# Dealing a routing stage's score products among other tiles, with a shorter per-layer gate, in a two-layer encoder kernel

## The chip, the cores and the metric

The kernel runs on one core of a Trainium2 chip. Its time is the device time of one execution in microseconds (us). The engines run side by side, each through its own queue in order: TensorE (PE, with its weight loads as PEld), VectorE (DVE), ScalarE (ACT), GpSimd (POOL) and SyncE (SP), which issues nearly all DMAs.

## What is computed

Two layers over 256 tokens of width 1024. Layer 0 mixes with a Mamba-2 block, layer 1 with retention; each is followed by a PEER expert FFN and a gated per-layer input. All matrices are float32. The FFN and the gate matter here:

```python
def peer_ffn(h, w_q, sub_keys, u, v):            # h: rms-normed
    q = (xt @ w_q).reshape(T, PEER_HEADS, 2, PEER_HALF)
    sc = jnp.einsum('thcd,hckd->thck', q, sub_keys)
    s1, i1 = lax.top_k(sc[:, :, 0], K)
    s2, i2 = lax.top_k(sc[:, :, 1], K)
    cand = (s1[..., :, None] + s2[..., None, :]).reshape(T, PEER_HEADS, K * K)
    ...
    gate = jax.nn.softmax(top_s, axis=-1)
    hid = jax.nn.gelu(jnp.einsum('tkd,td->tk', u[ib], xb), approximate=False)
    return jnp.einsum('tk,tkd->td', (gb * hid), v[ib])

h = h + peer_ffn(rms_norm(h, ffn_norm[i]), ...)
g = jax.nn.sigmoid(rms_norm(h, ple_norm[i]) @ ple_gate[i])
h = h + g * (p[i] @ ple_proj[i])
```

There are 16384 experts, 8 heads, 128 keys in each half and K = 16. The kernel doesn't gather experts: it multiplies all tokens with all of u, multiplies by a dense matrix of gates (zero where an expert isn't chosen), and multiplies with all of v.

## The kernel before

Every float32 product is made of three products in float32r: each operand is split into a high part (`wh`, `xh`: a cast on ScalarE) and the rest (`wl`, `xl`: a subtraction on VectorE or GpSimd). `get()` hands out the next split weight tile; it also starts the cast of the tile after that and the load of one further on. `wh` and `wl` have two buffers each, so a cast waits until TensorE is through with the tile two before.

The stages of a layer are the mixer, `peer` and `ple`. The program is written in the order in which each engine shall work; nothing reorders it.

`peer` runs these stages:

- Two q products of eight steps (`dense`), 1024 columns of q each. After a step `dense` calls a function with the step's number: in the second product `q_fill`, which issues a part of the selection (`pump`, 1550 ns of credit), moves x between partitions by DMA (steps 0 and 1) and splits x for the u tiles (steps 4 and 6). At the end four banks are evicted by VectorE (`q_evac`, L353).
- Scores: `score(tb, c4)` multiplies four of the 16 key halves for a block of 128 tokens into one PSUM tile (of two, `g`), and ScalarE copies it out (L995). Two of the eight calls stand between the two products, for q of the first product; six stand behind the second.
- The selection (`bg`, a list of pieces with costs): `sel_codes` takes the top 16 of two key halves on VectorE, for token block 0 and then block 1; sums, candidates, positions and gates follow, and at last `sel_tr`, which turns the gates on TensorE.
- u: 128 tiles. A tile's 128 rows are loaded, transposed by VectorE (L511), cast by ScalarE (L516), split by GpSimd (L519), and used in 24 products (L1237 to L1241) into a PSUM tile (of two, `m`). The loop issues selection pieces (`PUMP`) until the list is empty. From then on each tile also has a gate slot: `g_hot` (VectorE) and `g_lo` (ScalarE) make one-hot operands for four tokens, `g_mm` (L1183) multiplies them, `g_apply` (L1195, L1193) puts the gates of these tokens for all 128 tiles into `H`, and `gelu` (L1201, L1204, L1205) joins the activation to them. There are 64 such groups of four tokens.
- v: 128 steps (L1266). Four rows of `H` at once are split by `wsplit` into the operands for four steps.

`ple` forms p's projection (`pp`, scaled by 0.5), then the product with `ple_gate` (`dense` with `ends=2`: the last two steps run bank by bank, L213), with the norm's pieces issued from the table `FIRST_PLE` ("q", "Q", "t", "s": squares, sum, spread). The sigmoid is 0.5 + 0.5 tanh: `base` (L1335) adds `pp` to h on GpSimd during the product, `gated` (L1339) multiplies the tanh by `pp`, `added` (L1343) adds to h. Bank 0's `gated` and the first two `added` run on GpSimd, the others on VectorE.

Of the kernel before, what the change touches and what calls it, by code (L numbers as in the profile page):

```python
# [8 lines left out]
F32 = mybir.dt.float32  # L9
# [5 lines left out]
OP = mybir.AluOpType  # L15
# [3 lines left out]
P = 128  # L19
T = 256  # L20
# [4 lines left out]
GS = 4096.0  # L25
PUMP = 1700
UEND = 56
HPOOL = (0, 1)
GPOOL = (0,)

# [16 lines left out]
FIRST_SSD = ('aq', 't', 's', '', '0h', '1H', 'b', '')  # L49
FIRST_RET = ('', 'qQ', '', 'cbt', 'das0', '', 'h1', 'H')  # L50
FIRST_Q = ('q', 'Q', '', 't', 'sa', 'b', '', '')
FIRST_PLE = ('q', 'Q', '', 't', 'sa', 'bcd', '', '')
HEADS = 8
TOPK = 16

# [32 lines left out]
def trunk(ctx: ExitStack, tc: tile.TileContext, a, out, dbg=None, stop=None):  # L88
    nc = tc.nc
    pe, act, dve, pool, sp = nc.tensor, nc.scalar, nc.vector, nc.gpsimd, nc.sync  # L90
# [12 lines left out]
    hT = big.tile([P, KD, T], F32, name="hT")  # L103
# [17 lines left out]
    def place():  # L121
        v = X[:, xn[0] % 3]
        xn[0] += 1
        return v[:, 0], v[:, 1]
# [58 lines left out]
    def split_x(src, n=4):  # L183

        xh, xl = place()
        act.copy(xh[:, :n], src)  # L186
        dve.tensor_sub(xl[:, :n], src, xh[:, :n].bitcast(F32))
        return xh, xl
# [30 lines left out]
    def dense(xs, evac, pieces=lambda k: 0, m=2, ends=1):  # L219


        s = Acc()
        for k in range(KD - 2 if ends == 2 else KD):
            if xs is st0:
                xs.before(k)
            wh, wl = get()
            if isinstance(xs, Stream) and xs is not st0:
                xs.before(k)
            xh, xl = (xs.xs if isinstance(xs, Stream) else xs)[k]
            s.step(wh, wl, xh, xl, k == 0, m if k == KD - 1 else 0)  # L230
            if k < KD - 1:
                fill(pieces(k))
        if ends == 2:
            s.close([get(k < KD - 1) + xs.xs[k] for k in (KD - 2, KD - 1)])
        for b in range(4):
            evac(b, s.bank(b))
        fill(pieces(KD - 1))
# [143 lines left out]
    def first(st, xs, plan, *more):  # L381


        named = {"q": (st.squares, 0), "Q": (st.squares, 2), "t": (st.total,), "s": (st.spread,),
                 "0": (st.scaled, 0, xs), "h": (st.half, 0, xs), "1": (st.scaled, 1, xs), "H": (st.half, 1, xs)}
        for i, c in enumerate(more):
            named["abcdef"[i]] = c

        def f(k):
            todo[:0] = [named[c] for c in plan[k]]  # L390
            return len(plan[k])

        return f
# [552 lines left out]
    def peer(l, st):  # L946
        H = view(0, P, T)
# [41 lines left out]
        def score(tb, c4):  # L989
            ps = gps.tile([P, 512], F32, name="g")  # L990
            for j in range(4):
                c = 4 * c4 + j
                pe.matmul(ps[:, j * P:(j + 1) * P], qT[:, c, tb * P:(tb + 1) * P], kT[:, c], start=j == 0,
                          stop=True, skip_group_check=True)
            act.copy(sc[:, tb, 4 * c4:4 * c4 + 4], ps.rearrange("p (a b) -> p a b", a=4))  # L995
# [110 lines left out]
        def wait():  # L1106
            pass

        bg = [(3100, sel_codes, tb, c) for tb in range(2) for c in range(0, 16, 2)]
        for tb in range(2):  # L1110
            bg += [(1800, sel_sums, tb)]
            bg += [(2500, sel_cand, tb, h) for h in range(0, 8, 2)]
# [14 lines left out]
                fn(*x)  # L1127

        def q_fill(k):
            if bg[0][3] < 8:  # L1130
                pump(1550)
            if k < 2:
                q_move(2 * k)
                q_move(2 * k + 1)
            if k in (4, 6):
                xh, xl = split_x(xm[:, 2 * k - 8:2 * k - 4])
                xp.extend((xh[:, i], xl[:, i]) for i in range(4))
            return 0

        dense(st, q_evac(0), first(st, None, FIRST_Q, (normed, 0), (normed, 1)))  # L1140
        score(0, 0)
        score(0, 1)
        dense(st.xs, q_evac(8), q_fill)

        for c4 in (2, 3):
            score(0, c4)
        for c4 in range(4):
            score(1, c4)


        bank = [acc.tile([P, 512], F32, name="ps") for _ in range(4)]
# [35 lines left out]
        def g_apply(b, ps, i):  # L1187

            pv = ps.rearrange("p (t i) -> p i t", t=4)
            assert i >= UEND  # L1190
            hv = H[:, :, 4 * b:4 * b + 4]
            if i < P:
                act.activation(hv[:, i:], pv[:, i:], AF.Copy, scale=1.0 / GS)  # L1193
            if i:
                dve.scalar_tensor_tensor(hv[:, :i], pv[:, :i], 1.0 / GS, hv[:, :i], op0=OP.mult, op1=OP.mult)  # L1195
            stored[0] = 4 * b + 4

        def gelu(i, ps):
# [25 lines left out]
        for i in range(P):  # L1224
            wh, wl = get()
            if last is not None:
                g_slot(i, gelu(i - 1, last))
                if bg:
                    pump(PUMP)
                else:  # L1230
                    since += 1
                    if since % 8 == 0 and T // 4 - gst["next"] > P - 1 - i:
                        g_slot(i)
            last = mis.tile([P, 512], F32, name="m")[:, :T]
            for k, (xh, xl) in enumerate(xp):
                s = slice(k * P, (k + 1) * P)
                pe.matmul(last, wh[:, s], xh, start=k == 0, stop=False)  # L1237
                pe.matmul(last, wh[:, s], xl, start=False, stop=False)  # L1238
            for k, (xh, xl) in enumerate(xp):
                s = slice(k * P, (k + 1) * P)  # L1240
                pe.matmul(last, wl[:, s], xh, start=False, stop=k == KD - 1)  # L1241
        assert not bg

        def wsplit(j):
            return split_x(H[:, 4 * j:4 * j + 4])

        def open_():
            return gst["next"] < T // 4 or gst["lo"] or gst["mm"] or gst["ap"]
# [46 lines left out]
        pp = view(0, KD, T)  # L1295
# [28 lines left out]
    def ple(l, st, pp):  # L1324
        ga = view(2560, KD, T)
        st2 = Stream(COL["mix_norm"] + 8)
        if l:
            gfin, junk = view(16384, D), view(17408, T)
            fs = small.tile([P, 2, 4], F32, name="fs", bufs=1)
            sp.dma_start(gfin, a["final_norm"].partition_broadcast(P))  # L1330


        def base(b):
            hv = hT[:, 2 * b:2 * b + 2]
            pool.tensor_add(hv, hv, pp[:, 2 * b:2 * b + 2])  # L1335

        def gated(b):
            g = ga[:, 2 * b:2 * b + 2]
            (pool if b in GPOOL else dve).tensor_mul(g, g, pp[:, 2 * b:2 * b + 2])  # L1339

        def added(b):
            hv = hT[:, 2 * b:2 * b + 2]
            (pool if b in HPOOL else dve).tensor_add(hv, ga[:, 2 * b:2 * b + 2], hv)  # L1343
            if l == 0 and b < 3:
                st2.hi(2 * b)
                st2.hi(2 * b + 1)

        def turned_out(b):

            for tb in range(2):  # L1350
                o = ot[b // 2 * 2 + tb][:, b % 2 * T:b % 2 * T + T]
                for k in range(2):
                    pe.transpose(o[:, k * P:(k + 1) * P], hch[2 * b + k][:, tb * P:(tb + 1) * P], ident)
            for tb in range(2):
                o = ot[b // 2 * 2 + tb][:, b % 2 * T:b % 2 * T + T]
                act.activation(junk[:, :T], o, AF.Square, accum_out=fs[:, tb, b:b + 1])

        def g_evac(b, ps):
            g = ga[:, 2 * b:2 * b + 2]
            st.divide(g, ps)  # L1360
            if b == 3:
                prepare(True)
            act.activation(g, g, AF.Tanh, scale=0.5)
            if b == 1:
                gated(0)
            if b == 2:
                added(0)
                gated(1)
            if b == 3:
                added(1)  # L1370
                gated(2)

        if l == 0:
            keys = view(30464, 4, 512)
            for c4 in range(4):
                key_load(1, c4, keys[:, c4])
        dense(st, g_evac, first(st, None, FIRST_PLE, *((base, b) for b in range(4))), ends=2)
        if l == 0:
            tiles = [pool_.tile([P, 512], F32, name=n_) for pool_, n_ in ((gps, "g"), (gps, "g"), (mis, "m"), (mis, "m"))]
            for c4 in range(4):  # L1380
                key_turn(keys[:, c4], tiles[c4])
            st2.copies = [(key_copy, c4, tiles[c4]) for c4 in range(4)]
            st2.lo(0)
            st2.lo(1)
            ready.append(ready.pop()())
            prepare(True)
            added(2)
            gated(3)
            added(3)
            return st2  # L1390
        ot = [pool_.tile([P, 512], F32, name=n_) for pool_, n_ in ((gps, "g"), (gps, "g"), (mis, "m"), (mis, "m"))]
        added(2)
        turned_out(0)
        gated(3)
        added(3)
        for b in range(1, 4):
            turned_out(b)
        return ot, fs, gfin
# [26 lines left out]
    for j in range(2):  # L1425
        for tb in range(2):
            o = raws.tile([P, D], F32, name="raw")[:, :512]
            c = slice(512 * j, 512 * j + 512)
# [29 lines left out]
```

## Time and profile before

| | us |
|---|---|
| Runs shown | 2243.55, 2245.3, 2249.71 |
| Median | 2245.3 |
| Profiled execution | 2246.1 |
| Its span | 2244.2 |
| TensorE busy | 2165.3 (96%) |
| TensorE weight loads | 2006.2 (89%) |
| VectorE busy | 1563.2 (70%) |
| ScalarE busy | 1210.4 (54%) |
| GpSimd busy | 878.4 (39%) |

Durations in the rows come from the profiled execution. Its span runs from the first to the last instruction of the program, the 1.9 us around it belong to the execution. "Busy" is time in which an instruction of the engine ran; what an engine waited for is a view of its own. Layer 0's second q product begins at 299.18 us of the span, its u tiles at 332.69, v at 756.89; layer 1's u tiles begin at 1421.57, v at 1843.32.

### The profile page before, as it was taken

The numbers are of one execution on the slowest core, as the hardware profiler recorded it, in microseconds if no ns is written. First come the engines' busy times: TensorE is split into PE (matmuls) and PEld (weight loads), VectorE is DVE, ScalarE is ACT, GpSimd is POOL, SyncE is SP. The second block draws the span as 40 slices with busy tenths as digits, with TensorE's granted clock in tenths as the row PEclk, the third lists the DMA queues.
The fourth block names the chain that finished last, engine by engine and source line by source line (L and its number), as shares of the span: only waits on it lengthen the run. The fifth ranks groups of instructions, "written<-read, shape, count | busy, mean of one in ns | idle before, by whom it ended". The sixth has DMA issues, their size and how long they took to land. (4 is left out here: it accounts for less than half of the span.)

```text
span 2244.2 us, 39809 instructions
## 1 busy us (share of the span) xinstructions
PE 2165.3 (96%) x15013; PEld 2006.2 (89%) x15013; DVE 1563.2 (70%) x2625; ACT 1210.4 (54%) x2063; POOL 878.4 (39%) x408
## 2 busy tenths in 40 slices
PE   7899899999999999999989999999999999999997
PEld 7788899999999888888888999999999998888886
DVE  7478678887788655555587366889678875555556
ACT  4544444546888644444553444445588874444444
POOL 5743248886666200000044123788766640000002
PEclk9999999999999999999999999999999999999998
DMA  5432467756555555555645455776555545666653
GB/s 165 136 106 86 143 192 181 183 139 160 143 148 144 160 195 190 196 193 192 201 160 174 138 166 177 176 191 154 160 148 145 145 147 194 193 194 192 194 192 104
DMA packets 219577, 370.27 MB, mean 165 GB/s; under 512 B 24240, under 2 KB 163192, under 8 KB 219384
## 3 DMA queue, kind: packets, MB, share of 16 engines
q1 hardware_dynamic: 219064, 367.19, 55.0%
q8 instruction: 118, 1.93, 0.4%
q14 instruction: 75, 0.61, 0.1%
q10 hardware_dynamic: 320, 0.53, 0.1%
HBM read 364.48 MB, written 1.05 MB: 163 GB/s over the span
## 5 line engine op out<-in xcount | busy, mean ns | idle before, releaser
L135 ACT CAST wh<-raw 128x1024 fp32r<-128x1024 f32 x429 | 450.3, 1052 | 519.7 <-PE ps L1266 362.5
L138 DVE TENSOR_TENSOR wl<-raw,wh 128x1024 fp32r<-128x1024 f32 x365 | 453.6, 1246 | 393.9 <-ACT wh L135 393.9
L519 POOL TENSOR_TENSOR wl<-raw,wh 128x1024 fp32r<-128x1024 f32 x256 | 615.5, 2406 | 240.5 <-ACT wh L516 231.1
L1266 PE MATMUL ps<-wh,X 128*128 128x512 f32 x2048 | 509.2, 390 | 4.6 <-ACT X L186 4.6
L1237 PE MATMUL m<-X,wh 128*128 128x256 f32 x2048 | 512.9, 288 | 0.6 <-ACT arena L1201 0.6
L1238 PE MATMUL m<-X,wh 128*128 128x256 f32 x2048 | 501.8, 283 | 0.0
L1266 PEld LDWEIGHTS ps<-wh,X 128*128 128x128 f32 x2048 | 385.0, 188 | 85.3 <-ACT X L186 5.0
L516 ACT CAST wh<-raw 128x1024 fp32r<-128x1024 f32 x256 | 269.1, 1051 | 274.9 <-issue 157.1
L1237 PEld LDWEIGHTS m<-X,wh 128*128 128x128 f32 x2048 | 392.8, 192 | 1.2 <-ACT arena L1201 1.0
L1238 PEld LDWEIGHTS m<-X,wh 128*128 128x128 f32 x2048 | 391.2, 191 | 0.0
L198 PE MATMUL ps<-X,wh 128*128 128x256 f32 x2368 | 333.6, 291 | 14.7 <-ACT wh L135 8.4
L340 POOL TENSOR_TENSOR arena<-arena 128x512 f32<-128x512 f32 x15 | 22.5, 1502 | 825.2 <-ACT arena L338 824.8
L198 PEld LDWEIGHTS ps<-X,wh 128*128 128x128 f32 x2368 | 307.5, 197 | 20.7 <-ACT wh L135 10.4
L1241 PE MATMUL m<-X,wl 128*128 128x256 f32 x2048 | 287.4, 283 | 0.1
L1266 PE MATMUL ps<-wl,X 128*128 128x512 f32 x1024 | 274.7, 389 | 0.0
L1241 PEld LDWEIGHTS m<-X,wl 128*128 128x128 f32 x2048 | 264.1, 191 | 0.7 <-POOL wl L519 0.7
L1266 PEld LDWEIGHTS ps<-wl,X 128*128 128x128 f32 x1024 | 192.4, 188 | 40.1
L138 POOL TENSOR_TENSOR wl<-raw,wh 128x1024 fp32r<-128x1024 f32 x64 | 165.5, 2597 | 157.6 <-ACT wh L135 157.5
L511 DVE STREAM_TRANSPOSE raw<-raw 128x1024 f32<-128x1024 f32 x144 | 179.2, 1244 | 50.1 <-DMA raw<-in_peer_u 37.4
L198 PE MATMUL ps<-X,wl 128*128 128x256 f32 x1184 | 178.9, 289 | 15.6 <-POOL wl L138 8.0
L198 PEld LDWEIGHTS ps<-X,wl 128*128 128x128 f32 x1184 | 159.6, 196 | 18.0 <-DVE wl L138 9.0
L1177 ACT ACTIVATE ol<-oh,G 128x128 f16<-128x128 f16 x512 | 168.4, 401 | 1.5 <-PE g L1183 0.3
(263 smaller groups left out, 2158.9 us busy)
## 6 DMA issues: line engine op xcount, KB each, us to landing
raw<-in_peer_v SPq DMA_DIRECT2D x256, 512.0 KB, 4.3
raw<-in_peer_u SPq DMA_DIRECT2D x576, 128.0 KB, 3.0
arena<-in_peer_u SPq DMA_DIRECT2D x448, 128.0 KB, 3.3
raw<-in_ret_w_in SPq DMA_DIRECT2D x48, 512.0 KB, 4.1
raw<-in_ssd_w_in SPq DMA_DIRECT2D x41, 512.0 KB, 3.7
raw<-in_peer_w_q SPq DMA_DIRECT2D x32, 512.0 KB, 4.8
raw<-in_ssd_w_out SPq DMA_DIRECT2D x16, 512.0 KB, 3.6
raw<-in_ple_gate SPq DMA_DIRECT2D x16, 512.0 KB, 4.5
```

What stands on the lines that cost most here:

```text
L135: act.copy(wh[:, :n], r[:, :n])
L138: (eng or dve).tensor_sub(wl[:, :n], r[:, :n], wh[:, :n].bitcast(F32))
L198: pe.matmul(self.t[n // 2][:, n % 2], w[:, n * P:(n + 1) * P], x, start=st, stop=sp_, skip_group_check=True)
L340: pool.tensor_add(self.sq[:, 0], self.sq[:, 0], self.sq[:, b])
L511: dve.transpose(t.rearrange("p (k b i) -> p b k i", k=8, b=4), r.rearrange("p (b k i) -> p b k i", k=8, b=4))
L516: act.copy(wh, t)
L519: pool.tensor_sub(wl, t, wh.bitcast(F32))
L1177: act.activation(ol[:, j], oh[:, 0, :, j], AF.Copy, scale=G1[:, t:t + 1])
L1237: pe.matmul(last, wh[:, s], xh, start=k == 0, stop=False)
L1238: pe.matmul(last, wh[:, s], xl, start=False, stop=False)
L1241: pe.matmul(last, wl[:, s], xh, start=False, stop=k == KD - 1)
L1266: pe.matmul(sums[b], h[:, tb * P:(tb + 1) * P], w[:, n * 512:(n + 1) * 512], start=i == 0 and p == 0, stop=i == P - 1 and p == 2)
```

## The change

The change has three parts. Four of the scores are issued from `q_fill`, one after each of the first four steps of the second q product, and the other four after the first two u tiles; the list of selection pieces takes the lower half of the key halves of both token blocks first. `base` is gone: `gated` computes (tanh + 1) times `pp` in one operation and always runs on VectorE. The last group's gates are applied to the first four tiles in an operation of their own, and `wsplit(0)` splits the first row alone and then the other three.

```diff
-FIRST_PLE = ('q', 'Q', '', 't', 'sa', 'bcd', '', '')
+FIRST_PLE = ('q', 'Q', '', 't', 's', '', '', '')
...
-        bg = [(3100, sel_codes, tb, c) for tb in range(2) for c in range(0, 16, 2)]
+        bg = [(3100, sel_codes, tb, c0 + c) for c0 in (0, 8) for tb in range(2) for c in range(0, 8, 2)]
...
         def q_fill(k):
+            if k < 4:
+                score(k // 2, k % 2)
             if bg[0][3] < 8:
                 pump(1550)
...
-        score(0, 0)
-        score(0, 1)
         dense(st.xs, q_evac(8), q_fill)
-
-        for c4 in (2, 3):
-            score(0, c4)
-        for c4 in range(4):
-            score(1, c4)
...
             if i:
-                dve.scalar_tensor_tensor(hv[:, :i], pv[:, :i], 1.0 / GS, hv[:, :i], op0=OP.mult, op1=OP.mult)
+
+                for r in ((slice(0, 4), slice(4, P)) if 4 * b + 4 == T else (slice(0, i),)):
+                    dve.scalar_tensor_tensor(hv[:, r], pv[:, r], 1.0 / GS, hv[:, r], op0=OP.mult, op1=OP.mult)
...
                 pe.matmul(last, wl[:, s], xh, start=False, stop=k == KD - 1)
+            if i < 2:
+                score(i, 2)
+                score(i, 3)
...
         def wsplit(j):
-            return split_x(H[:, 4 * j:4 * j + 4])
+            if j:
+                return split_x(H[:, 4 * j:4 * j + 4])
+            xh, xl = place()
+            for r in (slice(0, 1), slice(1, 4)):
+                act.copy(xh[:, r], H[:, r])
+                dve.tensor_sub(xl[:, r], H[:, r], xh[:, r].bitcast(F32))
+            return xh, xl
...
-        def base(b):
-            hv = hT[:, 2 * b:2 * b + 2]
-            pool.tensor_add(hv, hv, pp[:, 2 * b:2 * b + 2])
-
         def gated(b):
             g = ga[:, 2 * b:2 * b + 2]
-            (pool if b in GPOOL else dve).tensor_mul(g, g, pp[:, 2 * b:2 * b + 2])
+            dve.scalar_tensor_tensor(g, g, 1.0, pp[:, 2 * b:2 * b + 2], op0=OP.add, op1=OP.mult)
...
-        dense(st, g_evac, first(st, None, FIRST_PLE, *((base, b) for b in range(4))), ends=2)
+        dense(st, g_evac, first(st, None, FIRST_PLE), ends=2)
```

The line numbers of the changed kernel differ by one to six. ScalarE's queue from the second q product to the first u tiles, before (`wh<-raw` at L135 is a cast for q, at L516 for u; `g` is a score, `m` a u tile):

```order
L995 COPY arena<-g 128x512 x2
L135 CAST wh<-raw 128x1024 x5
L186 CAST X<-arena 128x1024
L135 CAST wh<-raw 128x1024 x2
L186 CAST X<-arena 128x1024
L516 CAST wh<-raw 128x1024
L995 COPY arena<-g 128x512 x6
L516 CAST wh<-raw 128x1024 x2
L1201 ACT_TABLE_LOAD
L1201 ACTIVATE arena<-m 128x256
```

The same queue in the changed kernel, from the third dealt score on:

```order
L994 COPY arena<-g 128x512
L134 CAST wh<-raw 128x1024
L994 COPY arena<-g 128x512
L134 CAST wh<-raw 128x1024
L185 CAST X<-arena 128x1024
L134 CAST wh<-raw 128x1024 x2
L185 CAST X<-arena 128x1024
L515 CAST wh<-raw 128x1024 x2
L994 COPY arena<-g 128x512 x2
L515 CAST wh<-raw 128x1024
L1197 ACT_TABLE_LOAD
L1197 ACTIVATE arena<-m 128x256
```

A score's copy now stands ahead of a cast in each of the first four steps, and behind the product two casts of u come before the next copies.

VectorE's queue at the end of the u tiles, before (`arena<-g,arena` applies gates, to as many tiles by four tokens as the row says; `arena<-arena,m` joins the gelu; `X` is v's operand):

```order
L138 TENSOR_TENSOR wl<-raw,wh 128x1024
L1195 SCALAR_TENSOR_TENSOR arena<-g,arena 128x127x4
L1205 TENSOR_TENSOR arena<-arena,m 128x244
L1195 SCALAR_TENSOR_TENSOR arena<-g,arena 128x128x4
L1205 TENSOR_TENSOR arena<-arena,m 128x248
L1195 SCALAR_TENSOR_TENSOR arena<-g,arena 128x128x4
L187 TENSOR_TENSOR X<-arena,X 128x1024
```

The same place in the changed kernel:

```order
L137 TENSOR_TENSOR wl<-raw,wh 128x1024
L1191 SCALAR_TENSOR_TENSOR arena<-g,arena 128x127x4
L1201 TENSOR_TENSOR arena<-arena,m 128x248
L1191 SCALAR_TENSOR_TENSOR arena<-g,arena 128x4x4
L1191 SCALAR_TENSOR_TENSOR arena<-g,arena 128x124x4
L1201 TENSOR_TENSOR arena<-arena,m 128x252
L1249 TENSOR_TENSOR X<-arena,X 128x256
L1249 TENSOR_TENSOR X<-arena,X 128x768
```

The gates run one tile ahead of before, so that one of the two full applications behind the last tile is gone; the other is in two pieces, and the first cast and subtraction for v are 256 columns wide. On TensorE the last `g_mm` accordingly stands ahead of the last u tile instead of behind it.

GpSimd's queue in `ple` of layer 1, before:

```order
L257 TENSOR_TENSOR r_23999<-r_23999,mhalf 128x2
L1335 TENSOR_TENSOR hT<-hT,arena 128x512 x4
L1339 TENSOR_TENSOR arena<-arena 128x512
L1343 TENSOR_TENSOR hT<-arena,hT 128x512 x2
L1424 TENSOR_TENSOR r_24168<-r_24168,mhalf 128x2
```

In the changed kernel the rows of L1335 and L1339 are gone from it, and VectorE has one `gated` more, between the evictions of banks 1 and 2.

## Rows read from the trace of the kernel before

**Rows 1.** Waits of TensorE: line, its releaser: us in total, times, longest.
```profile
PE m L271 <- DVE dg L264: 8.7, 7, 2.8
PE g L993 <- DVE arena L353: 5.1, 2, 2.6
PE ps L1266 <- ACT X L186: 4.6, 2, 2.3
PE ps L213 <- DVE wl L138: 1.4, 4, 0.6
```

**Rows 2.** Timeline of TensorE, second q product: start, us, instruction, [idle before <-releaser].
```profile
297.47 1.95 PE L993 MATMUL g<-arena 128*128 128x128 f32 x16
299.18 2.16 PE L198 MATMUL ps<-X,wh 128*128 128x256 f32 x16
...
325.25 7.68 PE L993 MATMUL g<-arena 128*128 128x128 f32 x48 [2.58 <-DVE arena L353]
332.69 0.36 PE L1237 MATMUL m<-X,wh 128*128 128x256 f32 x1
```

**Rows 3.** Windows: stretch, us, TensorE busy (instructions), granted clock, DMA share, GB/s.
```profile
328.00:329.00 1.00, 1.00 (x7) 0.50 0.12 29
758.00:759.00 1.00, 1.00 (x4) 0.50 0.00 0
1844.00:1845.00 1.00, 0.94 (x5) 1.00 0.00 0
```

**Rows 4.** Window in u: us busy of PE, PEld, DVE, ACT, POOL; clock, DMA.
```profile
337.00:505.00 168.00, 168.00 (x1403) 168.00 (x1402) 145.25 (x434) 80.96 (x121) 140.53 (x59) 1.00 0.66 168
```

**Rows 5.** Timelines of VectorE and of GpSimd, end of the second q product.
```profile
320.99 2.48 DVE L187 TENSOR_TENSOR X<-arena,X 128x1024 fp32r<-128x1024 f32 x1
...
324.55 2.44 DVE L353 TENSOR_TENSOR arena<-ps,arena 128x512 f32<-128x512 f32 x4
...
309.46 10.50 POOL L138 TENSOR_TENSOR wl<-raw,wh 128x1024 fp32r<-128x1024 f32 x4 [1.25 <-ACT wh L135]
```

**Rows 6.** Timeline of TensorE, first steps of v, layer 0 and layer 1.
```profile
756.89 3.68 PE L1266 MATMUL ps<-wh,X 128*128 128x512 f32 x8 [2.27 <-ACT X L186]
...
761.34 2.00 PE L1266 MATMUL ps<-wh,X 128*128 128x512 f32 x8
...
764.08 1.98 PE L1266 MATMUL ps<-wh,X 128*128 128x512 f32 x8
...
1843.32 2.45 PE L1266 MATMUL ps<-wh,X 128*128 128x512 f32 x8 [2.28 <-ACT X L186]
...
1846.52 1.98 PE L1266 MATMUL ps<-wh,X 128*128 128x512 f32 x8
```

**Rows 7.** Timelines of ScalarE and of VectorE behind the last u tile, layer 0.
```profile
753.94 0.18 ACT L1201 ACTIVATE arena<-m 128x8 f32<-128x8 f32 x1 [1.61 <-PE m L1241]
754.15 0.36 ACT L1204 ACTIVATE m<-m 128x248 f32<-128x248 f32 x1
755.79 1.04 ACT L186 CAST X<-arena 128x1024 fp32r<-128x1024 f32 x1 [1.28 <-DVE arena L1195]
...
755.08 0.68 DVE L1195 SCALAR_TENSOR_TENSOR arena<-g,arena 128x512 f32<-128x512 f32 x1
```

**Rows 8.** Timelines of GpSimd, VectorE and TensorE in `ple`, layer 0; 1162.88 behind it.
```profile
1131.53 6.00 POOL L1335 TENSOR_TENSOR hT<-hT,arena 128x512 f32<-128x512 f32 x4
...
1131.60 2.54 DVE L264 TENSOR_SCALAR dg<-ident,r 128x128 f32<-128x128 f32 x2 [0.81 <-POOL r L257]
...
1162.88 0.48 DVE L264 TENSOR_SCALAR dg<-ident,r 128x128 f32<-128x128 f32 x2 [0.81 <-POOL r L257]
...
1134.19 0.49 PE L271 MATMUL m<-dg,ones 128*128 128x128 f32 x2 [0.41 <-DVE dg L264]
```

**Rows 9.** Timeline of VectorE: four operations with a scalar, two plain ones.
```profile
1165.74 1.67 DVE L359 SCALAR_TENSOR_TENSOR arena<-hT,par,arena 128x256 f32<-128x256 f32 x4 [1.24 <-ACT arena L350]
...
1179.81 0.75 DVE L809 TENSOR_TENSOR arena<-arena 128x256 f32<-128x256 f32 x2
```

More of the change, by code (lines that the diff above doesn't have):

```diff
@@ L28 @@
 HPOOL = (0, 1)
-GPOOL = (0,)
 SSD_ORDER = """
```

## The prediction

> **What bounds the kernel now.** I read the view of waits first, for TensorE alone, since the page has it busy 96% of the span: what can be won is where it stands still, and what follows a standstill. The reader should see that four waits of that list lie where the change works [rows 1]: the scores behind VectorE's eviction (5.1 us in two waits), the first step of the v phase behind ScalarE's cast (4.6 us in two), the spread of the norm behind `dg` (8.7 us, of which one small part is touched), and the closing steps of the per-layer product behind `wl` (1.4 us in four). Then I read the timeline around each, with the granted clock beside it, because the cost does not end with the wait. In layer 0 the scores start after 2.58 us of standstill [rows 2], and from then on a stretch ran at a granted clock of 0.50, which is 1.2 GHz instead of 2.4 [rows 3]. So a standstill is paid for twice. Between these places the u phase shows TensorE busy for 168.00 of 168 us, VectorE for 145.25 and GpSimd for 140.53 [rows 4]: there TensorE alone sets the pace, nothing moved off it is won, and nothing is lost by putting 0.86 us of scores between two tiles.
>
> The sum is made against the profiled execution, 2246.1 us, which is 0.8 us above the median of the three runs (2245.3) and inside their spread (2243.55 to 2249.71).
>
> **Scores dealt out.** From the first score, 297.47, to the first u tile, 332.69, layer 0 spends 35.22 us [rows 2]. In it are eight steps of the second q product, 299.18 to 322.67 (325.25 less the 2.58 waited), 23.49 us, and eight groups of four scores. The first two groups took 299.18 - 297.47 = 1.71 us, 0.86 each, so eight cost 6.84. 23.49 + 6.84 = 30.33, and 35.22 - 30.33 = 4.89 us are lost: 2.58 waiting, and 2.31 because the last six groups took 332.69 - 325.25 = 7.44 us at the lower clock instead of 5.13. The change keeps the steps and the scores, and puts nothing that waits behind the product: u tile 0 needs the second half of x, whose `xl` VectorE finished at 320.99 + 2.48 = 323.47 [rows 5], and a u tile. The eviction that was waited for (four pieces in 2.44 us from 324.55) then runs beside u tile 0, and scores (0, 2) want its first half only after that tile. The product itself now holds two groups more and lasts 1.71 us longer, while VectorE's queue in it has the same pieces in the same order, so VectorE is no later against TensorE than it was. What is left: in ScalarE's queue each dealt copy stands ahead of the cast for a later step, and GpSimd, which makes `wl` for this product, is busy without a pause over the last four steps, 10.50 us for four [rows 5], 2.6 us each against a step of 2.9. The last step wants its `wl` early, because it runs bank by bank. I bound this wait by nothing and 0.6 us and take 0.3. Gain 4.6 us. In layer 1 the wait is 5.1 - 2.58 = 2.5 us by the total [rows 1], and the pattern of scores is the same: 4.5 us. Together 9.1 us. The new order of the selection makes the condition in `q_fill` hold in the last step too, which leaves 1550 ns more of credit, and the gates begin one u tile earlier; the work is the same, and VectorE has 168 - 145 = 23 us free for it [rows 4].
>
> **Start of the v phase.** Because of that earlier tile the last gate product stands ahead of the last u tile and not behind it. Before, TensorE waited 2.27 us from the end of that product (754.62) to 756.89 [rows 6], on this chain [rows 7]: ScalarE's gelu on the last tile, VectorE's last gate multiplication (755.08, 0.68 us, 512 columns), the cast of four v inputs at once (755.79, 1.04 us). Now the gate's rows 0 to 3 are multiplied first, while the last u tile still runs, and the cast takes row 0 alone. ScalarE's queue remains: gelu at 753.94, its second part 754.15 to 754.51, then a cast of 256 columns, for which I take 0.36 us, from the 248 columns of 754.15. That puts v's first operand 0.93 us behind the start of the gelu, and TensorE starts 0.06 later, as it did after 755.79 + 1.04 = 756.83: 1.0 us of standstill, not 2.27. Its `xl` comes from VectorE behind the rest of the gate multiplication and the gelu product (0.7 + 0.4 us) and is bounded by no wait and 0.3 us.
>
> The other half is the clock. Layer 0's first v step took 761.34 - 756.89 = 4.45 us, the second 764.08 - 761.34 = 2.74: 1.71 us lost, at a granted clock of 0.50. Layer 1 waited 2.28 us and its first step took 1846.52 - 1843.32 = 3.20 us, with the clock at 1.00 [rows 3, 6]. So standstills of this length sometimes lower the clock and sometimes don't; I take it that one of 1.0 us alone does not. Gain: layer 0 1.27 + 1.71 = 3.0, layer 1 1.28 + 0.46 less 0.1 = 1.6, together 4.6 us.
>
> **The per-layer gate.** `base` is four additions on GpSimd, 6.00 us from 1131.53 [rows 8]. TensorE never waits for them, but VectorE slows beside them: two `dg` of 128x128 took 2.54 us there, and 0.48 at 1162.88, where GpSimd was still. TensorE waited 0.41 us for the second `dg` and, over both layers, 1.4 us for the `wl` behind it [rows 1, 8]. Without `base` these 1.8 us go, except where the cast, and not VectorE, is late: 0.3 per layer stays. Gain 1.2 us. The gate of bank 0 moves from GpSimd to VectorE, into a stretch where VectorE waits for the next bank; nothing there is later.
>
> Each `gated` becomes an operation with an immediate and two tensors in SBUF. The nearest rows are 128x256: four of that form in 1.67 us, 0.42 each, and two plain multiplications in 0.75, 0.38 each [rows 9]. So the new form costs between nothing and 0.1 us more for each of the eight; at the end of the kernel three stand on the path, 0 to 0.3 us, and I take 0. The Trainium skill's page "Vector Engine (DVE) Microarchitecture Reference", section "Points that are easy to get wrong", says that this form with two sources in SBUF that are not bf16 runs at half throughput; by an estimate from that page of the Trainium skill each of six near the path would cost some 0.5 us more, and the sum would be 2234. The row of 0.42 us speaks against it.
>
> **Sum.** 9.1 + 4.6 + 1.2 = 14.9; 2246.1 - 14.9 = 2231.2, and I give 2231.
>
> **Rivals.**
> 1. The standstill ahead of v still lowers the clock, or its first operand comes later than I count. 1.7 us for each layer come back, and up to 1 us of waiting: 2234.6 to 2236.6. For it: 2.27 and 2.28 us went different ways, so the length alone does not decide [rows 3, 6].
> 2. u tiles come late. TensorE reaches u tile 0 some 8 us sooner than before (332.69 against 297.47 + 23.49 + four groups = 324.4), while VectorE, which transposes every u tile, has the same work: if its lead is gone, the q gain of 9.1 us is waited for again and the time is 2240. Against it: VectorE is free 23 us of 168 in that phase.
> 3. Nothing comes of it: what TensorE saves at q is waited for at a later bound, within 7 us of before. Nothing in the trace names that bound.
> 4. Slower. The dealt score's copy holds up the cast queued behind it, and that `wl` on GpSimd (2.6 us each), so that steps of the second q product wait. Six steps in two layers can be hit; at 14.9 / 12 = 1.24 us a step the whole gain is gone; with GpSimd's piece wholly uncovered, 2.6 us, the time is 2246.1 - 14.9 + 31 = 2262. Against it: in the trace these steps ran 23.49 / 8 = 2.94 us with GpSimd just keeping up, and each dealt group gives it 0.86 us more.
> 5. The half rate of the immediate form, as a mechanism of this kernel: 512 columns take two times 0.38, twice that at half rate, so each of six multiplications near a path (three in each layer) is up to 0.76 us dearer, 4.6 us: 2235.8. The 0.42 us for 256 columns, which would be near 0.76, denies it [rows 9].
> 6. Better. Standstills elsewhere, which the change only shifts in time, fall so that they no longer lower the clock; at 1.7 us each two or three of them give 2226 to 2228.
>
> **How the numbers follow.** Forecast 0.64, with its own range 2227.5 to 2235; rival 1 0.13, rival 2 0.04, rival 3 0.04, rival 4 0.03, rival 5 0.02, rival 6 0.10. The unknown bounds (0.6 for `wl`, 0.3 for `xl`, 0.3 at the end) sum to 2 us upward; the clock, at two or three standstills that the change only shifts in time, is worth 1.7 us either way each. From 2226 to 2238 the range takes in forecast, rivals 1, 5 and 6. Faster by over 0.3% (6.7 us, about what a measurement of this kernel can tell from no change) are the forecast and rivals 1, 5 and 6: 0.89; within 0.3% rivals 2 and 3: 0.08; slower 0.03.
>
> **What would show it.** In the profile after, no wait of the scores for the eviction, and no stretch at 0.50 between q and u; the first u tile some 8 us earlier and the third about 5. At the start of v about 1 us of standstill and a first step of about 2.8 us in both layers. Two `dg` of the per-layer stage in about 0.5 us. TensorE's idle time down by about 9 us in all, the rest of the gain from the clock. The prediction is wrong if the second q product takes over 28 us from its first step, scores included, if u tiles wait for VectorE, or if a new standstill of 2 us appears.

## The result, and the profile after

The changed kernel took 2232.66 us (median of 5 runs, 2230.34 to 2236.84) beside 2246.93 for the kernel before: ratio 0.9942, interval 0.9927 to 0.9958, which is 13 us (9.4 to 16.4). The forecast was 2231.0 with a range of 2226 to 2238. The time was right. One of the terms behind it was far too large and a wait was left out, and most of what follows is about that.

The profiled execution of the changed kernel is the slowest of its five: 2236.84 us, span 2235.1. Against the one of before (2246.1, span 2244.2) it shows only 9.3 of the 14.9 us forecast.

Waits of TensorE in the changed kernel, the rows that answer to [rows 1]: line, releaser, us in total, times, longest.

```profile
PE ps L197 <- POOL wl L137: 9.0, 4, 4.5
PE m L270 <- DVE dg L263: 8.3, 6, 2.8
...
PE g L1177 <- DVE arena L1191: 3.6, 2, 2.0
...
PE ps L1271 <- ACT X L1248: 1.9, 2, 1.0
...
PE ps L212 <- DVE wl L137: 0.5, 2, 0.2
```

The scores' wait of 5.1 us is gone, v's fell from 4.6 to 1.9, the closing `wl` wait from 1.4 to 0.5. One row is new in size: `g_mm` (L1177) waits 3.6 us for `g_apply` (L1191). Before, that wait was 0.7 us:

```profile
PE g L1183 <- DVE arena L1195: 0.7, 2, 0.4
```

TensorE's timeline at the end of the second q product of layer 0, to be laid beside [rows 2]:

```profile
298.53 2.41 PE L197 MATMUL ps<-X,wh 128*128 128x256 f32 x16
...
322.62 0.64 PE L197 MATMUL ps<-X,wh 128*128 128x256 f32 x4
323.92 0.50 PE L197 MATMUL ps<-X,wl 128*128 128x256 f32 x2 [0.66 <-POOL wl L137]
...
326.17 0.40 PE L197 MATMUL ps<-X,wl 128*128 128x256 f32 x2
...
329.29 2.31 PE L992 MATMUL g<-arena 128*128 128x128 f32 x16
...
334.31 1.95 PE L992 MATMUL g<-arena 128*128 128x128 f32 x16
```

The product now runs into u tile 0 (326.41) without a break, and the two late pairs of scores stand between u tiles. The last step's wait for GpSimd's `wl`, taken as 0.3 us and bounded at 0.6, is 0.66, and 0.65 in layer 1.

TensorE's timeline at the start of v, layer 0 and layer 1, beside [rows 6]:

```profile
753.67 2.11 PE L1271 MATMUL ps<-wh,X 128*128 128x512 f32 x8 [0.97 <-ACT X L1248]
...
756.52 1.98 PE L1271 MATMUL ps<-wh,X 128*128 128x512 f32 x8
...
1837.22 2.11 PE L1271 MATMUL ps<-wh,X 128*128 128x512 f32 x8 [0.97 <-ACT X L1248]
...
1840.08 1.98 PE L1271 MATMUL ps<-wh,X 128*128 128x512 f32 x8
```

A standstill of 0.97 us in both layers and first steps of 2.85 and 2.86 us, as forecast (1.0 and 2.8). The granted clock stayed at 1.00 in both places, behind the q product and in v (beside [rows 3], 0.50 twice):

```profile
328.00:329.00 1.00, 1.00 (x11) 1.00 (x10) 1.00 (x3) 0.42 (x1) 0.00 (x0) 1.00 0.09 23
754.00:755.00 1.00, 1.00 (x6) 0.82 (x5) 0.89 (x2) 1.00 (x2) 0.00 (x0) 1.00 0.02 8
```

What was not forecast lies 200 us into u, where the gates begin. VectorE's timeline there, layer 0:

```profile
519.31 1.24 DVE L510 STREAM_TRANSPOSE raw<-raw 128x1024 f32<-128x1024 f32 x1
520.47 0.65 DVE L1163 TENSOR_TENSOR oh<-ps,G 128x1024 f16<-128x1024 f16 x1
521.15 0.42 DVE L1165 TENSOR_TENSOR oh<-oh,ps 128x512 f16<-128x512 f16 x1
523.09 1.25 DVE L510 STREAM_TRANSPOSE raw<-raw 128x1024 f32<-128x1024 f32 x1 [1.51 <-DMA raw<-in_peer_u]
524.26 0.65 DVE L1163 TENSOR_TENSOR oh<-ps,G 128x1024 f16<-128x1024 f16 x1
524.95 0.42 DVE L1165 TENSOR_TENSOR oh<-oh,ps 128x512 f16<-128x512 f16 x1
525.28 0.42 DVE L1191 SCALAR_TENSOR_TENSOR arena<-g,arena 128x260 f32<-128x260 f32 x1
```

TensorE's timeline beside it:

```profile
523.08 1.12 PE L1237 MATMUL m<-X,wl 128*128 128x256 f32 x8
525.76 0.29 PE L1177 MATMUL g<-oh 128*128 128x128 f16 x1 [1.56 <-DVE arena L1191]
```

And windows behind this standstill and behind the one of layer 1 (granted clock, then DMA share and GB/s, at the end of the row):

```profile
528.00:529.00 1.00, 1.00 (x7) 1.00 (x7) 0.31 (x3) 0.00 (x0) 0.00 (x0) 0.50 0.72 221
1610.00:1611.00 1.00, 1.00 (x6) 1.00 (x6) 0.97 (x4) 0.80 (x3) 0.71 (x1) 0.50 0.56 157
```

The first `g_apply` stands in VectorE's queue behind a transpose (L510) that waits 1.51 us for the load of its u tile. `g_mm` has two PSUM tiles and can go no further until `g_apply` has read one. In layer 1 the same chain gave 2.05 us. After both, TensorE ran at the lower level (1.2 GHz) for a stretch.

### The profile page after: what moved, and what is told of

Its sections match the earlier page's. It is cut to its first block, busy times and chain, and to the rows that moved or that the text cites. A ratio compares the mean times of both kernels' runs of the same rounds, so it can differ in the third digit from the quotient of the medians.

```text
span 2235.1 us, 39809 instructions
## 1 busy us (share of the span) xinstructions
PE 2163.1 (97%) x15013; PEld 2006.3 (90%) x15013; DVE 1554.6 (70%) x2633; ACT 1210.4 (54%) x2069; POOL 864.4 (39%) x398
## 5 line engine op out<-in xcount | busy, mean ns | idle before, releaser
L510 DVE STREAM_TRANSPOSE raw<-raw 128x1024 f32<-128x1024 f32 x144 | 179.2, 1244 | 48.3 <-DMA raw<-in_peer_u 34.6
```

The source lines that it names most:

```text
L510: dve.transpose(t.rearrange("p (k b i) -> p b k i", k=8, b=4), r.rearrange("p (b k i) -> p b k i", k=8, b=4))
```

## The experiments

A stage table was made from the starts in TensorE's timelines: "q" is from the end of the first q product to the fourth u tile, by which time all eight scores are done in every version; "u" from there to the first product of v, the standstill ahead of v included; "v1" the first v step. Each pair is layer 0, layer 1, in us.

| Profile | q | u | v1 | span |
|---|---|---|---|---|
| before | 43.9, 44.2 | 415.5, 413.0 | 4.45, 3.20 | 2244.2 |
| before, again | 44.4, 42.4 | 414.0, 414.3 | 4.78, 4.42 | 2244.3 |
| per-layer gate alone | 40.8, 40.2 | 414.7, 413.3 | 4.69, 4.40 | 2234.6 |
| v start alone | 44.4, 42.5 | 413.0, 414.2 | 2.87, 2.85 | 2240.1 |
| scores alone | 40.1, 40.1 | 414.8, 413.9 | 3.20, 3.21 | 2238.0 |
| changed | 40.4, 40.1 | 414.7, 415.7 | 2.85, 2.86 | 2235.1 |
| changed, again | 40.4, 40.1 | 413.3, 414.6 | 2.85, 2.85 | 2229.4 |

**One part at a time.** The scores alone: the kernel before with

```diff
+            if k < 4:
+                score(k // 2, k % 2)
```

in `q_fill`, the other four behind u tiles 0 and 1, and the new order of `bg`.

> The kernel before with the dealt scores and the new order of the selection alone; the per-layer gate and the start of v are as before. In the two profiles at hand the q stages (first score to fourth u tile) shrank by 3.5 and 4.1 us, and the gates, which start a tile earlier, had a new standstill of 1.6 and 2.1 us at the first g_mm, each with a stretch of lower clock behind it (1.7 us each). Theory (the earlier gate start makes that standstill in every execution): g_mm waits for VectorE's g_apply for over 2 us in all again, and the time is 2246.9 - 7.6 + 5.0 - 1.0 for v (the last gate product now ahead of the last u tile) = about 2243. Rival (the standstill belonged to that one execution): that wait is under 1 us and the time is about 2238.

Ratio 0.9982 (0.9973 to 0.9991): 4.0 us (2.0 to 6.1), not the 9.1 forecast. `g_mm` waited 2.5 us, so the standstill at the gates came again, this time without a lower clock. The theory holds in the wait. The kernel before took 2243.37 us in these runs, so the time is to be taken as a difference: it fits the theory's 3.9 us, though without the lower clock that the theory counted in, and not the rival's 8.9.

The per-layer gate alone:

```diff
-            (pool if b in GPOOL else dve).tensor_mul(g, g, pp[:, 2 * b:2 * b + 2])
+            dve.scalar_tensor_tensor(g, g, 1.0, pp[:, 2 * b:2 * b + 2], op0=OP.add, op1=OP.mult)
```

and no `base`.

> The kernel before with the shorter per-layer gate alone. Theory: only the waits around it go (1.2 to 1.3 us; the two dg take about 0.5 us instead of 2.5), so about 2245.6, not to be told from no change by the median, but seen in the trace: first per-layer product step to the end of the span 43.5 us before in layer 1, 42.2 here with the clock as before, 40.8 if no stretch of it runs at the lower clock. Rival (the immediate form runs at half rate): gated takes 0.7 us or more for 512 columns more than the plain multiplication, and the end of the kernel is not earlier.

Ratio 0.9988 (0.9977 to 0.9999): 2.7 us (0.2 to 5.2), more than the 1.2 forecast, which the interval still holds. The waits went as forecast (`dg` 8.7 to 8.3, closing `wl` 1.4 to 0.5 us), and layer 1 took 41.0 us from the product's first step to the end, near the 40.8 of an undisturbed clock. But this profile brought something else. It is the kernel before up to the end of layer 0's v, yet its scores hardly waited:

```profile
PE ps L1266 <- ACT X L186: 4.5, 2, 2.3
...
PE g L993 <- DVE arena L353: 0.3, 2, 0.2
```

**Why the scores waited, or did not.** This called for a second profile of the kernel before, unchanged.

> The kernel before once more, unchanged, for a second profile of it. Theory (the wait of the scores for the eviction belongs to some executions only: VectorE's subtraction of 1024 columns beside GpSimd took 3.2 and 2.5 us in the profile shown, 1.4 and 1.3 us in the profile of the kernel with the per-layer gate alone, which is the same up to there): the wait is either 0.2 to 0.4 us in all, with subtractions of 1.3 us, or 5 us with subtractions of 2.5 us or more; never one without the other. Rival (the wait is part of every execution of this kernel, and the other kernel moved it): 5 us again with the subtractions whatever they are. Time: the same as before, ratio 1.000 within 0.0015.

The wait was 5.0 us again. VectorE's second subtraction for x and its eviction in that run, layer 0 (start, us, instruction):

```profile
321.19 3.36 DVE L187 TENSOR_TENSOR X<-arena,X 128x1024 fp32r<-128x1024 f32 x1
...
325.64 1.84 DVE L353 TENSOR_TENSOR arena<-ps,arena 128x512 f32<-128x512 f32 x3
```

GpSimd's split of u tile 0 at the same time, same run:

```profile
321.08 2.39 POOL L519 TENSOR_TENSOR wl<-raw,wh 128x1024 fp32r<-128x1024 f32 x1
```

The same two engines in the kernel with the per-layer gate alone, VectorE first:

```profile
319.45 1.29 DVE L187 TENSOR_TENSOR X<-arena,X 128x1024 fp32r<-128x1024 f32 x1
320.66 1.23 DVE L511 STREAM_TRANSPOSE raw<-arena 128x1024 f32<-128x1024 f32 x1
321.82 2.44 DVE L353 TENSOR_TENSOR arena<-ps,arena 128x512 f32<-128x512 f32 x4
```

```profile
319.62 3.38 POOL L519 TENSOR_TENSOR wl<-raw,wh 128x1024 fp32r<-128x1024 f32 x1
```

Where GpSimd began 0.11 us ahead, VectorE's operation took 3.36 us and GpSimd's 2.39; where VectorE began 0.17 us ahead, 1.29 and 3.38. In each pair one operation runs at its own pace, and the other is longer by about the time for which it had to wait. The Trainium skill's page "SBUF — State Buffer", section "SBUF: two separate sides", says that when a VectorE operation with two SBUF inputs meets a GpSimd operation that reads SBUF, whichever starts first has the port pair that the two engines share for the whole instruction, and the other blocks; these rows agree. In the profile shown ahead of the prediction [rows 5] it was GpSimd that came first (319.99 against 320.99; the subtraction took 2.48). Over both layers of the four profiles of this q code, GpSimd was first in three and the scores waited 5 us; VectorE was first in one and they waited 0.3.

Is it the eviction's lateness alone? One line of the kernel before tells, by sending the selection piece that stands ahead of that subtraction behind the eviction (`dense` calls `q_fill` for step 7, the last, only after it):

```diff
-            if bg[0][3] < 8:
+            if k != 6 and bg[0][3] < 8:
```

> The kernel before with one line changed: the selection piece of step 6 of the second q product is issued behind the eviction instead of ahead of x's second subtraction. Nothing is dealt out. In four profiles of this q code the scores waited 5.0 us in three (VectorE's second subtraction began 0.1 to 1.0 us after GpSimd's split for u tile 0 and took 2.5 to 3.4 us), and 0.3 us in one (it began 0.1 to 0.2 us ahead of it and took 1.2 to 1.3). Theory (which of the two engines starts first decides, and the queued piece of 2.3 us makes VectorE late): the second subtraction begins some 1 us ahead of GpSimd's split, takes about 1.3 us, the scores wait under 0.6 us in all, first score to fourth u tile takes 40.2 to 40.9 us in both layers, and the time is 4 to 7 us under before, ratio 0.997 to 0.998. Rival (the eviction is late for another reason, the order of the selection is not it): the wait stays at 3 us or more and the ratio at 0.999 to 1.001.

The scores waited 0.3 us, q took 40.9 and 40.2 us, and the ratio was 0.9983 (0.9973 to 0.9992): 3.8 us, the same as dealing the scores (0.9982). The theory's detail fell, though. The subtraction still took 3.35 us in layer 0, because it now began inside GpSimd's piece before; it was the place in the queue that mattered:

```profile
317.36 1.25 DVE L511 STREAM_TRANSPOSE raw<-arena 128x1024 f32<-128x1024 f32 x1 [3.56 <-DMA arena<-in_peer_u]
318.52 3.35 DVE L187 TENSOR_TENSOR X<-arena,X 128x1024 fp32r<-128x1024 f32 x1
321.80 1.23 DVE L511 STREAM_TRANSPOSE raw<-arena 128x1024 f32<-128x1024 f32 x1
322.96 2.44 DVE L353 TENSOR_TENSOR arena<-ps,arena 128x512 f32<-128x512 f32 x4
```

**The start of v alone:** the two splits (in `g_apply` and `wsplit`) on the kernel before.

> The kernel before with the split of the last gate application and of v's first operands alone; gates start as before, so the last gate product stands behind the last u tile. Theory (each standstill of 2.27 us ahead of v mostly lowers the clock, one of 1.1 us never does): a standstill of about 1.1 us in both layers, first v steps of 2.85 us, and 2 x 1.15 + 1.5 x 1.8 = 5 us faster by the median, ratio 0.9978. Rival (the clock falls there in few executions, so that only the standstill is won): 2.3 us, ratio 0.9990. This kernel is the one before up to the end of u, so its profile also is a third look at the scores' wait, with the two outcomes as in the run of the kernel before.

Ratio 0.9973 (0.9962 to 0.9984): 6.1 us (3.6 to 8.5), against 4.6 forecast. The theory held: standstills of 1.12 us, first steps of 2.87 and 2.85. The stage table says where the surplus is. Over four profiles with the standstill of 2.27 us (before, before again, the gate alone, the one-line run: eight starts) the first step took 4.25 to 4.78 us in seven and 3.20 in one. The one that kept the clock was layer 1 of the profile that the forecast was made from.

**Where the gates begin.** The changed kernel once more:

> The changed kernel once more, unchanged, for a second profile of it and a time beside its variants. Theory (the standstill of 1.6 to 2.1 us at the first gate products comes with the queue order, not with one execution): the wait of g_mm for g_apply is 2 to 4 us over both layers again, and a lower clock behind it in none, one or both. Rival (an accident of the profile shown): under 1 us. Time: ratio 0.992 to 0.996.

2229.77 us, ratio 0.9928 (0.9911 to 0.9945). `g_mm` waited 3.0 us, so it is no accident of one profile. But the clock stayed at 1.00, even behind the 2.25 us of layer 1; its rows, standstill and windows:

```profile
1604.35 0.29 PE L1177 MATMUL g<-oh 128*128 128x128 f16 x1 [2.25 <-DVE arena L1191]
```

```profile
1605.00:1606.00 1.00, 1.00 (x11) 1.00 (x10) 1.00 (x2) 0.74 (x3) 1.00 (x1) 1.00 0.89 255
1606.00:1607.00 1.00, 1.00 (x10) 1.00 (x10) 0.85 (x4) 0.58 (x2) 0.54 (x1) 1.00 0.53 146
```

Then the start of the gates was moved, by the cost of the piece `wait`, a tile later (3550 instead of 2000, the tile of before) and a tile earlier (300).

> The changed kernel with the cost of the piece `wait` raised from 2000 to 3550, which takes the extra credit of 1550 back: the gates start at the same tile as in the kernel before, and the last gate product stands behind the last u tile again. Theory (the earlier start made the new standstill at the first g_mm): that standstill is gone (under 1.5 us in all over both layers, no stretch of lower clock there), v waits about 1.7 us instead of 0.97, and the time is at or below the changed kernel's, 2229 to 2233. Rival (the standstill has to do with the shift of the u tiles against the selection, not with the tile at which the gates start): it stays at 3.6 us in all, and the time is 2235 to 2238.

> The changed kernel with the cost of the piece `wait` lowered from 2000 to 300, so that the gates start one u tile earlier still. With the later start the wait of g_mm for g_apply was 2.5 us, with the changed kernel's 3.6. Theory (any start close behind tile 56, from which the loads of u have two buffers fewer ahead of them, meets a transpose that waits for its load): 2 to 4.5 us again, ratio 0.993 to 0.997. Rival (it is the one tile): over 5 us or under 1 us.

Later: 2.5 us at `g_mm`, 1.12 ahead of each v instead of the 1.7 expected, ratio 0.9952 (0.9939 to 0.9965). Earlier: nothing at `g_mm` (the rival's figure), no standstill ahead of v and first steps of 2.74 us, but TensorE waited at `sel_tr` for the selection's last pieces, ratio 0.9933 (0.9916 to 0.9949):

```profile
PE g L1100 <- DVE arena L1069: 3.8, 2, 2.4
```

My theory for the later start fell: at the old tile the wait was 2.5 us and not under 1.5, while in the unchanged kernel it is 0.7 and 1.6 us. So the tile alone doesn't decide. That it also depends on which loads are late just then, and that this shifts with everything ahead, is likely but not shown. What makes the wait was settled by the queue. `g_apply` ahead of `get()` in the changed kernel:

```diff
         for i in range(P):
+            if gst["ap"]:
+                g_apply(*gst["ap"], i - 1)
+                gst["ap"] = None
             wh, wl = get()
```

> The changed kernel with g_apply issued ahead of get() in each u tile, so that in VectorE's queue it stands ahead of the tile's transpose, which waits for a load, and covers one tile fewer. Theory (g_mm waits because g_apply stands behind a transpose that waits for its load): the wait of g_mm for g_apply goes from 3.6 to under 0.7 us, no stretch of lower clock there, and the time is 2 to 6 us below the changed kernel's, 2227 to 2231. Rival (the loads are late themselves, so that TensorE waits for the u tile instead): a wait of the u tile's products for wl takes its place, and the time stays at 2231 to 2235.

No wait of `g_mm` is left. In its place u tiles waited 1.4 us for the two parts of the gelu, and not, as the rival had it, for a load. Ratio 0.9939 (0.9926 to 0.9951), 2231.27 us: the cause is shown, but no gain can be told from the changed kernel (0.9942 and 0.9928).

**Putting it together.** Three edits of the gates (`g_apply` first, a tile earlier, `sel_tr` behind the tile's products) and the last `wl` of the second q product on VectorE:

```diff
+            for k in range(KD):
+                weights(a["peer_w_q"][l], g * D, (g + 1) * D, k, k + 1, eng=pool if g and k < 7 else None)
```

> The changed kernel with four edits: g_apply ahead of get(), the gates one tile earlier still, the transposes of the selection (sel_tr) behind the tile's products instead of ahead of them, and `wl` of the last step of the second q product made by VectorE. Theory (what is left in the changed kernel are the waits of 0.66 us in each q product, 2.5 to 3.6 us at the first gate products or, with the earlier start, 3.8 us at sel_tr, and 0.97 us ahead of each v): those go, 5 to 7 us and perhaps a stretch of lower clock, ratio 0.989 to 0.9915. Rival (each standstill removed is waited for again, by u tiles whose loads are late): the ratio stays at 0.992 to 0.995.

Ratio 0.9939 (0.9925 to 0.9954), the rival's figure, but not by the rival's way. The gates' waits went (u 411.4, 411.0), and the edit of `wl` undid it: VectorE's second subtraction queued behind it, u tile 0 waited 1.76 us in both layers, at a lower clock from then on, and q took 42.7 us.

```profile
PE m L1239 <- DVE X L186: 3.5, 2, 1.8
```

The same without dealing, with the one-line edit in its place:

> The kernel before with everything but the dealt scores: the selection piece behind the eviction (as in the one-line run), the shorter per-layer gate, the split of v's start, and the gate edits of the combined run (g_apply ahead of get(), gates two tiles earlier than before, sel_tr behind the products). Theory (dealing the scores is worth no more than keeping the eviction early; the stage takes 40.1 us dealt and 40.2 to 40.8 undealt): within 1.5 us of the combined run, ratio 0.9895 to 0.992. Rival (dealing is worth the 9 us that were forecast): 6 us or more above the combined run, ratio above 0.993.

Ratio 0.9941 (0.9926 to 0.9956), within the 1.5 us of the combined run; both are above the range given, for the combined run's own mishap and because `sel_tr` here waited 3.5 us. That the two times agree says little, since the combined run lost some 5 us in q; what bears the theory out is that q took 40.8 and 40.0 us undealt. Last, the three edits of the gates alone on the changed kernel:

> The combined run without its edit of `wl` in the second q product, so the changed kernel with the three edits of the gates alone (g_apply ahead of get(), gates a tile earlier, sel_tr behind the tile's products). In the combined run the u stage took 411.4 and 411.0 us, against 413.3 to 415.7 in two profiles of the changed kernel, and v began without a standstill, but both q stages took 42.7 us instead of 40.1 to 40.4, since u tile 0 waited 1.8 us for VectorE's second subtraction, queued behind the new `wl`. Theory (the two are independent): q back to 40.1 us, u at 411 to 412, a span 5 us below the combined run's and a ratio of 0.990 to 0.992. Rival (u was short there because it started late, with its loads ahead): u back at 413 to 415 us, ratio 0.993 to 0.995.

2227.42 us (2224.36 to 2228.45), ratio 0.9920 (0.9906 to 0.9933), the best of all; q 40.1 and 40.1, u 411.1 and 412.0, span 2224.7, which is 8.4 under the combined run's instead of 5. The theory held. Against the changed kernel (0.9942 and 0.9928) the intervals overlap, so the 4.9 and 1.8 us between the ratios are likely a gain, but not a shown one.

## Why the time was right and the sum was not

| Term | forecast | alone, by runs |
|---|---|---|
| scores dealt | 9.1 | 4.0 (2.0 to 6.1) |
| start of v | 4.6 | 6.1 (3.6 to 8.5) |
| per-layer gate | 1.2 | 2.7 (0.2 to 5.2) |
| sum | 14.9 | 12.8 |
| the whole change | | 13.0 and 16.2 (two sets of runs) |

The three rows are not disjoint. With the scores alone the gates also begin a tile earlier, and in that run v began after standstills of 2.06 us with first steps of 3.20 and 3.21 us. Against the eight starts named above (2.27 us, first steps of 4.37 on the mean) that is 2.8 of the 4.0 us, by an estimate from these rows. So dealing as such, together with the wait at the gates that came with it, gave less than its row says, and a sum near the whole is no check of the parts.

**Scores.** The step that failed is "what is left" after 30.33 us of work. In the pair of profiles q shrank by 43.9 - 40.4 = 3.5 and 44.2 - 40.1 = 4.1 us, 7.6 of the 9.1: the `wl` wait was 0.66 instead of 0.3 in each layer, and the rest is small change at each switch between scores and product. The larger error was to take 2.58 us of standstill, and the low clock behind it, as a property of the kernel. It was the outcome of a race within 1 us between two engines, and in one profile of four the same code needed 40.8 and 40.2 us. Against that outcome dealing gains 0.4 and 0.1 us.

The race itself is still there. In layer 0 of the changed kernel GpSimd began first again, and VectorE's subtraction took 2.89 us. VectorE, GpSimd and the first product that reads the result:

```profile
324.42 2.89 DVE L186 TENSOR_TENSOR X<-arena,X 128x1024 fp32r<-128x1024 f32 x1
```

```profile
323.83 2.40 POOL L518 TENSOR_TENSOR wl<-raw,wh 128x1024 fp32r<-128x1024 f32 x1
```

```profile
327.49 0.28 PE L1234 MATMUL m<-X,wh 128*128 128x256 f32 x1
```

The prediction took it as done before u tile 0. It ended at 327.31, 0.9 us behind that tile's start and 0.18 us ahead of its reader (0.20 in the second profile; 2.5 in layer 1). Nothing waits for the eviction any more, but in layer 0 the second half of x was only just in time.

**A new standstill.** "The gates begin one u tile earlier; the work is the same, and VectorE has 23 us free for it" priced the move at nothing. It was read from an average over 168 us. What counted was the order in VectorE's queue at one place: a transpose that waits for its load, with `g_apply` behind it and TensorE behind that. It cost 2.5 to 3.6 us of waiting in the four profiles with dealt scores and this queue order (three with the new start of the gates, one with the old), where five profiles with the scores undealt had 0.5 to 1.6. The prediction named it as a sign of being wrong ("a new standstill of 2 us"), and the 2.05 us of layer 1 are one. The profiled execution is also dearer than the second profile of the same kernel, 5.7 us of span: 2.5 of that lie in u, where only the first lost the clock, 1.6 ahead of the first q product and 1.5 between v and layer 1's q.

**Start of v.** Mechanism and standstill were right (0.97 us each, clock never lowered in the ten starts of 0.97 to 1.12 us). By an estimate from the eight starts (2.27 and 4.37 us against 0.97 and 2.85) the term should have been 5.6 us instead of 4.6: layer 1's first step of 3.20 us was taken as its rule, and it is the exception among eight. The interval of the run with this part alone holds both figures.

**Per-layer gate.** Right within what can be measured. The immediate form is not at half rate: 512 columns in 0.68 us, as a plain operation of that size (0.69, both for L352, with one source in PSUM, and for L1344, with both in SBUF), and 1.17 to 1.39 us beside GpSimd's additions. That rules out rival 5. VectorE's timeline at the end of the changed kernel:

```profile
2219.06 0.69 DVE L352 TENSOR_TENSOR arena<-ps,arena 128x512 f32<-128x512 f32 x1 [0.74 <-PE ps L212]
2219.66 0.68 DVE L1340 SCALAR_TENSOR_TENSOR arena<-arena 128x512 f32<-128x512 f32 x1
...
2224.20 0.69 DVE L1344 TENSOR_TENSOR hT<-arena,hT 128x512 f32<-128x512 f32 x1
```

Of the other rivals, 1 (v's standstill still lowers the clock), 2 and 4 didn't come: u tiles were not late, and no step of the second product stalled but the last. The product took 27.9 us, just under the 28 that the prediction had set as a sign of being wrong. Rival 3 is out too, since the gain of 9.4 us or more is beyond its 7; whether rival 6 had a share was not told apart. So the forecast was right partly by luck: the scores' term was 5 us too large (3 us above the end of its interval), and the other two came out 1.5 us above the forecast each, which their intervals don't tell from none. A whole of 13.0 or 16.2 us fits the 14.9 all the same.

## What to carry to other kernels

A wait in one profile is one draw. Before it is priced, look whether its releaser is late for a reason that the program fixes or for one that a few tenths of a microsecond decide, and compare it with other occurrences. Here the other layer gave the 3.20 us of v away, but it agreed about the scores (2.58 and 2.5 us of waiting), and only the profile of another kernel with the same q code showed a wait of 0.3. Where a change moves work earlier, read the queue of the engine that does it, row by row at that place, for an instruction ahead of it that waits on a transfer; free time on average says nothing of that. And look for the cheaper edit: one queued piece moved behind the eviction gained as much as eight scores dealt out.

## What was not expected of the hardware

VectorE's 128x1024 subtraction of two tensors took 1.22 us by its median and up to 3.4 us, longer where an operation of GpSimd was still running when it began, and GpSimd's for a u tile took 2.4 us, or 3.4 where VectorE's was. Standstills of about the same length went both ways with the granted clock: 2.25 us at the gates left it at 1.00 and 1.56 us lowered it to 0.50; 2.27 us ahead of v lowered it in seven starts of eight, and 2.06 us there in neither layer. Length alone does not decide, and what does was not settled here.
